# A reserve in the list scheduler for operations of attention and out-projection whose operands are not yet there

## The chip, the cores and the metric

The kernel runs on one core of a Trainium2 chip. The core has five engines that work side by side, each through its own instruction stream in the order in which the program was written: TensorE (PE: matmuls, and the weight loads that the profile lists as PEld), VectorE (DVE), ScalarE (ACT), GpSimd (POOL) and SyncE (SP, which here issues the DMAs). The metric is the device time of one execution in microseconds.

## What is computed

One layer of a hybrid decoder for 1024 tokens of width 1024, in fp32, cut here to its skeleton:

```python
xn = rms_norm(x, norm1_g)
proj = xn @ w_in                                   # ONE input projection
q, k, v, p_rw = jnp.split(proj, [512, 1024, 1536], axis=-1)
attn = dilated_attention(q, k, v, ...)             # 8 heads; windows (128,1) (512,4) (2048,16)
attn = rms_norm(attn, attn_out_g)                  # per head
rwkv = rwkv7_time_mix(p_rw, ...)                   # 8 heads; a recurrence over the tokens
mixed = jnp.concatenate([attn, rwkv], axis=-1)
x = x + mixed @ w_out                              # ONE out-projection
xn2 = rms_norm(x, norm2_g)
x = x + (silu(xn2 @ w_gate) * (xn2 @ w_up)) @ w_down
```

## The kernel before

All large products are split into a high and a low half in a reduced fp32 type and made of three passes of 128x512 matmuls (high x high, high x low, low x high). In the program's names an "h" or "l" at the end of a tile is such a half: `woh`, `wol` are the out-projection's weights, `mh`, `ml` the transposed mixed rows, `oph`, `opl` feed-forward weights, `B11h`, `B21h` the normalised rows of the feed-forward part.

The program is not written in the order in which it runs. Each piece of work is a generator (a *stream*) with a rank; it yields operations, waits on marks, and requests for PSUM banks. The class `Flow` keeps a model clock for each engine, and for each tile the model time at which it is written and read. `ready` (line 180) gives the earliest model time r at which the head of a stream can start: not before its engine is free, and not before its operands are there. `run` takes, at every step, the stream with the smallest r; where several could start by the model's present time, the one of the lowest rank. `issue` moves the clocks on and `emit` (line 235) writes the instruction down. So every engine instruction of the profile has the line L235, and what runs in which order is the outcome of this choice. On the chip each engine then works its list strictly in that order and waits at the head of it.

The program goes through these stages (times from the start of the span):

- **0 to about 550 us.** The input projection (rank 9), and beside it the preparation and the RWKV recurrence (ranks 3 to 3.6). The recurrence is a serial chain: 8 pairs of heads ("units"), 8 chunks each; on PE one step is `chain<-S,ra`, `chain<-Rb,M`, `chain<-VS,kbT`, `chain<-Ub,M`, with short DVE and ACT operations between.
- **550 to 600.** The input projection is done; the recurrence of the last unit runs beside the first attention items. `attend` (ranks 8.2 and up, several workers) takes a group of query blocks at a time: scores `<-kk,qv` on PE, bias and maximum on DVE, exponentials on ACT (`sb`), transposes `<-cs,sb`, copies to `pt`, `<-pt,vv` on PE.
- **600 to 770.** Attention, and the first of 384 out-projection matmuls (`outproj`, rank 9.5) as work that can stand in between. The out-projection has 16 blocks of 24 matmuls: round 0 (blocks 0 to 7) takes the RWKV half of the mixed rows, round 1 (blocks 8 to 15) the attention half. `mix_T` (rank 7.7) transposes the rows of a block on PE and splits them on ACT and DVE into `mh`, `ml`; `add_up` (7.8) adds a block to `acc` on DVE.
- **770 to 845.** `finish` (7.9) normalises the attention rows, a part at a time on ACT, DVE and POOL; round 1 needs it. Behind the last part of it `norms2` and `combine` (8.05) make the eight row blocks of the feed-forward's input.
- **845 to the end.** The feed-forward part (ranks 20 and above).

Of the kernel before, what the change touches and what calls it, by code (L numbers as in the profile page):

```python
# [48 lines left out]


LATE, SWITCH = 300, 100
OWN = {"PE": 0, "ACT": 100, "DVE": 130, "POOL": 95, "SP": 900}


# [49 lines left out]
class Flow:  # L104
# [73 lines left out]
                self.scan(s.head)  # L178

    def ready(self, s):  # L180
        op = s.head
        if isinstance(op, Wait):
            if any(m not in self.marks for m in op.marks):
                return None
            return max((self.marks[m] for m in op.marks), default=0.0)
        if isinstance(op, Get):
            t, n = sorted(self.free[op.kind].values()), op.n or 1
            return t[n - 1] if len(t) >= n else None
        r = self.clk.get(op.eng, 0.0)
        if op.eng == "SP":  # L190
            r = max(r, self.clk.get("queues", 0.0) - 3000)
        for keys, which in ((op.rd, 0), (op.wr, 0), (op.wr, 1)):
            for k in keys:
                if k in self.slots:
                    for e, t in self.slots[k][which].items():
                        if e != op.eng or (e == "SP" and (keys is op.rd or which)):
                            r = max(r, t + LAG[e] + (60 + LATE if op.eng == "PE" else 0))
                        elif keys is op.rd and which == 0:
                            r = max(r, t + OWN[e])
        return r  # L200

    def issue(self, s, r):
# [34 lines left out]
    def run(self, until):  # L237
        while True:
            best = None
            for s in self.streams:  # L240
                self.advance(s)
            held = {}
            for s in self.streams:
                if s.done:
                    continue
                r = self.ready(s)
                if r is None:
                    continue
                if isinstance(s.head, Op):
                    eng = s.head.eng  # L250
                    if eng in held and max(r, self.now) + s.head.cost > held[eng]:
                        continue
                    if eng in HOLD and s.rank == 3.1 and self.now < r <= self.now + HOLD[eng]:
                        held[eng] = min(r, held.get(eng, r))
                if best is None or r < best[0]:
                    best = r, s
                    if r <= self.now:
                        break
            self.streams = [s for s in self.streams if not s.done]
            if all(s.done for s in until):  # L260
                return
            assert best, [(s.gen.__name__, s.head.marks) for s in self.streams if isinstance(s.head, Wait)]
            self.now = max(self.now, best[0])
            self.issue(best[1], best[0])


@with_exitstack
# [1592 lines left out]
```

## Time and profile before

| | us |
|---|---|
| three runs | 1490.73, 1492.36, 1492.68 |
| their median | 1492.36 |
| the profiled execution | 1501.24 |
| its span (first to last instruction) | 1499.4 |
| PE busy in the span | 1426.3 (95%) |
| DVE, ACT, POOL busy | 801.1, 714.3, 539.8 |

The profile comes from one execution, whose own time is 8.9 us above the median of the runs. A row of the trace has the start of an instruction, its length, engine and line, the operation with output and inputs, and in brackets the time the engine sat idle before it and what ended that. Rows of equal instructions in a run are joined (x4). The granted clock of PE is given as a share of 2.4 GHz.

### The profile page before, as it was taken

The page shows a single profiled execution, that of the slowest core. Times are in us where ns is not written, and L with a number is a line of the kernel's source. Part 1 is how long each engine was busy: PE and PEld are TensorE (multiplying, and loading weights), DVE is VectorE, ACT ScalarE, POOL GpSimd, SP SyncE. Part 2 cuts the span into 40 slices and gives each one's busy share as a digit, 9 for nine tenths or more (in the row PEclk, how much of TensorE's full clock was granted, in tenths as well). Part 3 has the DMA queues.
Part 4 walks back from the last instruction along what each step waited for, and adds up shares of the span by engine and source line. Part 5 has one row for each costly group of instructions (what it writes and reads, how often), then busy time and mean ns, then how long its engine had stood idle before and what let it go on. Part 6 is the DMA issues. An engine that isn't in the chain of part 4 may idle for free. (4 is left out here: it accounts for less than half of the span.)

```text
span 1499.4 us, 24765 instructions
## 1 busy us (share of the span) xinstructions
PE 1426.3 (95%) x8710; PEld 1155.9 (77%) x8710; DVE 801.1 (53%) x1799; ACT 714.3 (48%) x1768; POOL 539.8 (36%) x564
## 2 busy tenths in 40 slices
PE   8999989999999986799999899999999999999999
PEld 5677767777778865688888678888888888888887
DVE  5456677657656337666776734443444434334334
ACT  5434556576676775555855433333333333333332
POOL 4432344255645451422454733444444440000000
PEclk8999999999999988799999999999999999999999
DMA  5343222323323344998521222222222224445443
GB/s 192 108 120 75 65 82 78 99 76 110 115 87 103 105 150 125 276 248 224 151 63 50 84 78 85 85 83 79 75 79 80 85 77 134 148 148 197 148 148 126
DMA packets 199789, 173.83 MB, mean 116 GB/s; under 512 B 39025, under 2 KB 150897, under 8 KB 199666
## 3 DMA queue, kind: packets, MB, share of 16 engines
q1 hardware_dynamic: 199666, 172.26, 38.3%
q8 instruction: 69, 1.13, 0.3%
q14 instruction: 54, 0.44, 0.1%
HBM read 130.26 MB, written 37.75 MB: 112 GB/s over the span
## 5 line engine op out<-in xcount | busy, mean ns | idle before, releaser
L235 ACT ACTIVATE oph<-fraw 128x512 fp32r<-128x512 f32 x208 | 126.3, 627 | 228.7 <-PE chain L235 97.9
L235 POOL TENSOR_TENSOR opl<-fraw,oph 128x512 fp32r<-128x512 f32 x76 | 99.6, 1315 | 220.6 <-PE bank L235 71.3
L235 DVE TENSOR_TENSOR opl<-fraw,oph 128x512 fp32r<-128x512 f32 x132 | 87.5, 689 | 143.6 <-ACT oph L235 143.6
L235 ACT ACTIVATE oph<-sw 128x512 fp32r<-128x512 f32 x80 | 50.6, 632 | 179.4 <-DVE sw L235 71.5
L235 POOL TENSOR_TENSOR inlo<-inraw,inhi 128x512 fp32r<-128x512 f32 x62 | 82.2, 1326 | 84.8 <-ACT inhi L235 70.6
L235 PE MATMUL bank<-opl,oph 128*128 128x512 f32 x176 | 68.5, 389 | 0.0
L235 PE MATMUL bank<-oph 128*128 128x512 f32 x176 | 68.5, 389 | 0.0
L235 PE MATMUL bank<-oph,opl 128*128 128x512 f32 x176 | 68.5, 389 | 0.0
L235 DVE TENSOR_TENSOR opl<-sw,oph 128x512 fp32r<-128x512 f32 x80 | 56.0, 699 | 21.0 <-ACT oph L235 17.2
L235 DVE TENSOR_TENSOR uu<-bank,uu 128x512 f32<-128x512 f32 x20 | 13.8, 692 | 81.7 <-PE bank L235 81.7
L235 DVE SCALAR_TENSOR_TENSOR S<-chain,ec,Sp 64x64 f32<-64x64 f32 x112 | 31.6, 282 | 43.1 <-PE chain L235 38.5
L235 ACT ACTIVATE Ub<-chain 64x64 f32<-64x64 f32 x128 | 28.2, 220 | 54.6 <-DVE VS L235 52.4
L235 POOL TENSOR_TENSOR sw<-fraw 128x512 f32<-128x512 f32 x40 | 52.0, 1299 | 0.0
L235 ACT ACTIVATE Y<-chain 64x64 f32<-64x64 f32 x128 | 26.9, 212 | 51.1 <-DVE S L235 45.8
L235 ACT ACTIVATE inhi<-inraw 128x512 fp32r<-128x512 f32 x62 | 38.7, 624 | 16.7 <-DMA inraw<-in_w_in_dram 6.7
L235 DVE COPY Rb<-chain 64x64 f32<-64x64 f32 x128 | 28.9, 226 | 27.9 <-PE chain L235 25.4
L235 POOL TENSOR_TENSOR up<-up,sg 128x512 f32<-128x512 f32 x20 | 32.3, 1617 | 30.1 <-POOL sw L235 16.1
L235 ACT ACTIVATE sb<-sb,mx 128x256 f32<-128x256 f32 (+3 forms) x64 | 36.2, 567 | 14.4 <-DVE mx L235 14.3
L235 PEld LDWEIGHTS bank<-oph,opl 128*128 128x128 f32 x176 | 33.0, 188 | 6.9
L235 PEld LDWEIGHTS bank<-oph 128*128 128x128 f32 x176 | 33.0, 188 | 6.8
L235 PEld LDWEIGHTS bank<-opl,oph 128*128 128x128 f32 x176 | 33.0, 188 | 6.8
L235 POOL TENSOR_TENSOR rsf<-smf,nhalf 128x8 f32<-128x8 f32 x16 | 26.6, 1662 | 31.6 <-DVE smf L235 31.3
(494 smaller groups left out, 4228.6 us busy)
## 6 DMA issues: line engine op xcount, KB each, us to landing
fraw<-in_w_down_dram SPq DMA_DIRECT2D x88, 256.0 KB, 2.8
inraw<-in_w_in_dram SPq DMA_DIRECT2D x62, 256.0 KB, 2.9
fraw<-in_w_gate_dram SPq DMA_DIRECT2D x48, 256.0 KB, 3.7
fraw<-in_w_up_dram SPq DMA_DIRECT2D x48, 256.0 KB, 3.0
fraw<-h_d SPq DMA_DIRECT2D x44, 256.0 KB, 2.9
h_d<-up SPq DMA_DIRECT2D x42, 256.0 KB, 2.1
rkv_d<-stage SPq DMA_DIRECT2D x24, 256.0 KB, 2.9
xt<-in_x_dram SPq DMA_DIRECT2D x8, 512.0 KB, 7.3
```

The costliest lines, as they stand in the source:

```text
L235: op.fn(*op.a, **op.k)
```

## The change

For an operation of a stream with a rank from 7 up to (not including) 10, on any engine but SP, whose operands come later than its engine is free, `ready` notes a second number, `when`, 400 ns behind r. `run` compares streams by `when`, where there is one, and by r otherwise; what is chosen is still issued at r. So out of several operations the one whose operands are there already is taken before one whose operands come within the next 400 ns of model time, and before one whose operands came in the model after its engine fell free. Ranks 7 to 10 are the loads of the out-projection's weights, `mix_T`, `add_up`, `finish`, `norms2`, `combine`, `attend`, the input projection and the out-projection. The recurrence (3 to 3.6) and the feed-forward streams (20 and above) have no reserve of their own, and no wait or bank request has one.

```diff
@@ -49,6 +49,8 @@
 LATE, SWITCH = 300, 100
+
+SLACK, SLACKED = 400, (7, 10)
 OWN = {"PE": 0, "ACT": 100, "DVE": 130, "POOL": 95, "SP": 900}
@@ -178,7 +180,9 @@
     def ready(self, s):
+
         op = s.head
+        s.when = None
@@ -186,7 +190,7 @@
-        r = self.clk.get(op.eng, 0.0)
+        r = free = self.clk.get(op.eng, 0.0)
@@ -197,6 +201,8 @@
+        if op.eng != "SP" and SLACKED[0] <= s.rank < SLACKED[1] and r > free:
+            s.when = r + SLACK
         return r
@@ -252,16 +258,17 @@
-                if best is None or r < best[0]:
-                    best = r, s
-                    if r <= self.now:
+                when = s.when or r
+                if best is None or when < best[0]:
+                    best = when, s, r
+                    if when <= self.now:
                         break
@@
-            self.now = max(self.now, best[0])
-            self.issue(best[1], best[0])
+            self.now = max(self.now, best[2])
+            self.issue(best[1], best[2])
```

The number of instructions of each engine is the same; their order differs, and with it which PSUM bank a product takes (the names `bank`, `mm`, `chain` at the left). Three places follow. In these rows `emit` has the line L235 before and L241 after.

First, PE in the last unit of the recurrence, at its fifth chunk: from `VS,kbT` to the next `S,ra`, the first twelve of the 22 rows that this is before:

```order
L235 MATMUL chain_6507<-VS,kbT 128x128
L235 MATMUL chain_6507<-Ub_116,M 128x128
L235 MATMUL bank_6597<-cs,sb_6444 128x128 x2
L235 MATMUL bank_6610<-pt_6577,vv 64x256
L235 MATMUL bank_6610<-pt_6577,vv 128x256
L235 MATMUL bank_6610<-pt_6577,vv 64x256
L235 MATMUL bank_6622<-cs,sb_6446 128x128 x3
L235 MATMUL mm_6632<-cs,sb_6447 128x128 x4
L235 MATMUL bank_6658<-cs,sb_6447 128x128 x3
L235 MATMUL bank_6610<-pt_6611,vv 128x256
L235 MATMUL bank_6610<-pt_6611,vv 64x256
L235 MATMUL bank_6610<-pt_6611,vv 128x128
```

and the same stretch, whole, after:

```order
L241 MATMUL chain_6501<-VS,kbT 128x128
L241 MATMUL chain_6501<-Ub_116,M 128x128
L241 MATMUL mm_6585<-cs,sb_6441 128x128 x2
L241 MATMUL bank_6608<-pt_6583,vv 128x256
L241 MATMUL bank_6608<-pt_6583,vv 64x256
L241 MATMUL bank_6608<-pt_6583,vv 128x256
L241 MATMUL bank_6608<-pt_6583,vv 64x256
L241 MATMUL chain_6588<-S_111,ra 128x128
```

Of 33 attention instructions that stood between the two steps 6 are left; the others stand in the next two steps of the recurrence and, 17 of them, behind its last instruction.

Second, PE behind the last instruction of attention, where `mix_T` transposes the rows of out-projection block 12 (`cs,O`). Before, the end of block 10, then the transposes, then block 11 (of 24 matmuls, whose first two are shown), behind which block 12 comes:

```order
L235 MATMUL mm_9181<-woh_8911,mh 128x512
L235 MATMUL mm_9181<-wol_8912,mh 128x512
L235 MATMUL mm_9181<-woh_8911,ml 128x512
L235 MATMUL bank_9212<-cs,O_6437 128x128
L235 MATMUL bank_9212<-cs,O_6438 128x128
L235 MATMUL bank_9212<-cs,O_6439 128x128
L235 MATMUL bank_9212<-cs,O_6440 128x128
L235 MATMUL mm_9207<-woh_8772,mh 128x512
L235 MATMUL mm_9207<-wol_8773,mh 128x512
```

After: the end of block 11, the transposes of blocks 12 and 13, and at once block 12:

```order
L241 MATMUL chain_9182<-wol_8703,mh 128x512
L241 MATMUL chain_9182<-woh_8702,ml 128x512
L241 MATMUL mm_9218<-cs,O_6434 128x128
L241 MATMUL mm_9218<-cs,O_6435 128x128
L241 MATMUL mm_9218<-cs,O_6436 128x128
L241 MATMUL mm_9218<-cs,O_6437 128x128
L241 MATMUL bank_9236<-cs,O_6434 128x128
L241 MATMUL bank_9236<-cs,O_6435 128x128
L241 MATMUL bank_9236<-cs,O_6436 128x128
L241 MATMUL bank_9236<-cs,O_6437 128x128
L241 MATMUL bank_9245<-woh_8547,mh 128x512
```

Between the last instruction of attention and the first matmul of block 12 there stood 60 out-projection matmuls (36 of them ahead of the transposes of block 12); now there are 10, all ahead of the transposes. Of the 384 matmuls 228 stood ahead of the end of attention, and 278 do now.

Third, PE at the end of the out-projection, where `norms2` transposes the normalised rows (`cs,nxn`) and the first feed-forward matmul (`B11h,oph`) follows. Before, the last of these transposes, with out-projection matmuls on both sides:

```order
L235 MATMUL chain_9473<-wol_8826,mh 128x512
L235 MATMUL mm_9483<-cs,nxn_9422 128x128 x4
L235 MATMUL chain_9473<-woh_8825,ml 128x512
L235 MATMUL chain_9473<-woh_8875,mh 128x512
L235 MATMUL chain_9473<-wol_8876,mh 128x512
```

After:

```order
L241 MATMUL mm_9473<-wol_8703,mh 128x512
L241 MATMUL mm_9473<-woh_8702,ml 128x512
L241 MATMUL chain_9489<-cs,nxn_9452 128x128 x4
L241 MATMUL bank_9498<-cs,nxn_9478 128x128 x4
L241 MATMUL bank_9510<-cs,nxn_9452 128x128 x4
L241 MATMUL bank_9519<-cs,nxn_9478 128x128 x4
L241 MATMUL chain_9549<-B11h,oph 128x512 x4
```

Before, 31 out-projection matmuls stood between the last transposes of `norms2` and the feed-forward's first matmul; now the transposes of the last two row blocks stand directly ahead of it.

## Rows read from the trace of the kernel before

**Rows 1.** The page: busy time, share, count; the chain that ended last.

```profile
PE 1426.3 (95%) x8710; PEld 1155.9 (77%) x8710; DVE 801.1 (53%) x1799; ACT 714.3 (48%) x1768; POOL 539.8 (36%) x564
...
PE 41%; DVE 0%; issue 0%
```

**Rows 2.** Table of windows: PE, PEld, DVE, ACT, POOL busy; PEclk, DMA share, GB/s.

```profile
900.00:1000.00 100.00, 100.00 (x437) 81.76 (x436) 41.21 (x64) 31.89 (x52) 40.69 (x32) 1.00 0.26 79
...
540.00:600.00 60.00, 41.82 (x234) 34.56 (x233) 35.62 (x115) 36.96 (x131) 13.31 (x14) 0.83 0.42 124
600.00:660.00 60.00, 50.91 (x288) 43.16 (x288) 38.84 (x132) 33.94 (x106) 22.97 (x23) 0.85 0.97 273
660.00:770.00 110.00, 103.78 (x679) 90.53 (x679) 81.21 (x293) 76.31 (x242) 43.16 (x80) 0.94 0.65 166
770.00:811.00 41.00, 41.00 (x207) 33.95 (x206) 27.24 (x49) 19.50 (x36) 16.71 (x27) 1.00 0.23 65
811.00:845.00 34.00, 26.98 (x132) 21.38 (x130) 27.47 (x34) 21.84 (x43) 24.90 (x21) 0.97 0.24 75
...
840.00:860.00 20.00, 16.02 (x64) 12.62 (x65) 15.74 (x22) 8.47 (x16) 15.25 (x12) 0.83 0.26 77
```

**Rows 3.** Timeline, end of the recurrence: start, length, engine, operation [idle before].

```profile
576.09 0.29 DVE L235 SCALAR_TENSOR_TENSOR S<-chain,ec,Sp 64x64 f32<-64x64 f32 x1
...
579.26 0.38 PE L235 MATMUL chain<-S,ra 128*128 128x128 f32 x2
...
600.08 0.48 PE L235 MATMUL chain<-cs,sb 128*128 128x128 f32 x1 [5.43 <-ACT sb L235]
```

**Rows 4.** Timeline of PE, 678 to 746: its waits for a head's queries.

```profile
689.01 1.39 PE L235 MATMUL mm<-kk,qv 128*128 128x128 f32 x6 [2.03 <-DMA qv<-qh_d]
...
745.32 0.66 PE L235 MATMUL chain<-kk,qv 128*128 128x128 f32 x4 [1.81 <-ACT qv L235]
```

**Rows 5.** Timeline of PE at the end of attention.

```profile
769.08 0.40 PE L235 MATMUL chain<-wol,mh 128*128 128x512 f32 x1
769.31 0.40 PE L235 MATMUL chain<-woh,ml 128*128 128x512 f32 x1
769.54 0.38 PE L235 MATMUL bank<-cs,sb 128*128 128x128 f32 x2
```

**Rows 6.** Timelines of DVE, PE and ACT: `finish`, then transposes and split of block 12.

```profile
772.06 0.29 DVE L235 TENSOR_TENSOR O<-O,agb 128x128 f32<-128x128 f32 x1
...
775.53 0.28 DVE L235 TENSOR_TENSOR O<-O,agb 128x128 f32<-128x128 f32 x1
...
778.48 0.60 PE L235 MATMUL bank<-cs,O 128*128 128x128 f32 x4
...
779.11 1.08 ACT L235 ACTIVATE mh<-bank 128x512 fp32r<-128x512 f32 x1 [4.84 <-PE bank L235]
...
780.23 1.10 DVE L235 TENSOR_TENSOR ml<-bank,mh 128x512 fp32r<-128x512 f32 x1 [0.28 <-ACT mh L235]
```

**Rows 7.** Timelines of ACT, DVE and PE: `norms2`, `combine`, first feed-forward products.

```profile
788.25 0.60 ACT L235 ACTIVATE B11h<-chain 128x512 fp32r<-128x512 f32 x1 [1.15 <-PE chain L235]
...
789.20 0.69 DVE L235 TENSOR_TENSOR B11l<-chain,B11h 128x512 fp32r<-128x512 f32 x1
...
811.33 1.10 PE L235 MATMUL bank<-B11h,oph 128*128 128x512 f32 x4
...
812.14 2.47 DVE L235 SCALAR_TENSOR_TENSOR nxn<-acc,nrs,g2bc 128x1024 f32<-128x1024 f32 x2
...
837.00 0.63 PE L235 MATMUL mm<-cs,nxn 128*128 128x128 f32 x4 [2.33 <-DVE nxn L235]
...
844.99 1.22 PE L235 MATMUL chain<-T1h,oph 128*128 128x512 f32 x2 [3.98 <-ACT T1h L235]
```

## Prediction

> **What bounds the kernel now.** I read the page first, then the table of windows, then PE's timeline where that table shows PE idle. The page has PE busy for 1426.3 of 1499.4 us, and the chain that ended last is all PE [rows 1]; so the time is PE's work plus PE's idle time, and an order that changes neither changes nothing. The table of windows says where idle time is left [rows 2]. From 900 to 1000 us PE is busy for 100.00 of 100 at a granted clock of 1.00 (2.4 GHz), and this is so for nearly all of the feed-forward part: nothing can be had there. Idle time stands in four stretches. 540 to 600 (18.2 us idle, clock 0.83) is the last unit of the serial recurrence. 600 to 660 (9.1 us, clock 0.85) has the DMA engines at 0.97: heads come in no faster than they are carried. 660 to 770 (6.2 us, clock 0.94) is attention proper. From 770 to 811 PE has no idle time at all, since the out-projection's rest fills it; from 811 to 845 it has 7.0 us.
>
> The change touches nothing but the order. In the feed-forward part it leaves the streams' own order as it is, so I cost that part at nothing; its cover is PE's own queue, which there never runs dry [rows 2].
>
> **The change, part by part.**
>
> *The dense stage, 0 to 550.* Counted in the order, the PE work between one step of the recurrence and the next, converted with the lengths of the rows, is 1.74 us before and 1.75 after ahead of `Rb`, 2.21 and 2.22 ahead of `VS,kbT`, 2.42 and 2.38 ahead of `S,ra` (means over some 53 steps each). Those differences, times 53, are 0.5 and 0.5 us of loss and 2.1 of gain. Value 0; bounds -1 and +2.
>
> *The last unit of the recurrence.* The state `S` of the fifth chunk is finished at 576.09 + 0.29 = 576.38, but its matmul starts at 579.26 [rows 3]: it stood behind the 33 attention instructions of the first fence, so 2.9 us were lost there. Now 6 stand there. That is a gain of 2.9 at most. It is not that much: the other instructions stand in the next two steps, or behind the chain, and there are three places at which an ACT or DVE operation of attention now stands ahead of one of the recurrence, each of the size of an ACT or DVE row of a few tenths, 1 us together. Also the chain's end does not release PE: after it PE waits 5.43 us for the first `sb`, until 600.08 [rows 3], and that waits for DVE to end the post-processing of the recurrence. The 17 instructions that now stand behind the last step fall into this hole and cost nothing there. I take -0.6, near nought, since most of what left one step comes back in the next two; bounds -2.9 and +1.
>
> *Attention, 660 to 770.* 50 out-projection matmuls (278 - 228) move ahead of the end of attention. One takes 769.31 - 769.08 = 0.23 us of PE [rows 5], so 11.4 us of work is put into this stage. By itself that makes attention end 11.4 us later and leaves 11.4 us less behind it: no gain. It gains what idle time it fills. The idle time there is 110.00 - 103.78 = 6.2 us [rows 2], and more than half of that is two waits for queries that have just been loaded, 2.03 and 1.81 us [rows 4]; ahead of the first stand matmuls of a later block now, and ahead of the second, scores of another head, so both can be filled. Against a full gain: the gaps that the order leaves in dependent work are not longer. From the last `pt,vv` of an item to its next transposes the PE work in between is 1.44 us before, 1.40 after, on the mean of 40; from transposes to their `pt,vv` 1.96 and 1.92, of 32. The additional matmuls went into gaps from scores to transposes (7.34 to 9.04), which were long enough. So I count the two waits and some 0.5 us besides, -4.4; bounds -6.2 (all idle time) and 0 (as much is lost at new heads of queues). 600 to 660 I leave at nought, the same number of matmuls standing ahead of its waits.
>
> The clock: at 0.94 on the mean over 110 us between 1.2 and 2.4 GHz, 0.06 x 2 x 110 = 13 us ran at the lower level [rows 2], which costs at most half of that, 6.6 us. PE falls there after waits: the 20 us from 840, which begin with a wait of 3.98 us, have 0.83 [rows 2, 7]. I give the clock no term, with 0 and -6.6 for its bounds, since the gaps do not get shorter. The Trainium skill (TensorE: Matmul & The Clock Gate, "HAM oscillation") says that bursts of matmuls with waits in between lose the high clock again and again, and that a steadier supply keeps it. The trace agrees as far as those 20 us go; by that rule the term would be -4.4 - 6.6 = -11.0 if the supply became steady, and a new hole elsewhere would cost more than its length.
>
> *Behind attention: block 12.* The last attention instruction on PE is that of 769.54 [rows 5]. Block 12 needs a part of `finish`, its transposes, and the split into `mh` and `ml`. Before, 36 matmuls, 8 us, ran ahead of its transposes and 24 more behind them: everything was hidden. Now 10 matmuls, 2.3 us, stand ahead, and none behind. The split shows fully: from the transposes at 778.48 to the end of `mh` at 780.19 are 1.7 us, to the end of `ml` 2.9 [rows 6]; the transposes of block 13 cover 0.6 and two matmuls 0.5 more. That is some 1.2 us at least. In addition the transposes of block 13 stand ahead of block 12 and need the next part of `finish`, which came 775.53 + 0.28 - 769.54 = 6.3 us after the end of attention [rows 5, 6]; less 2.3 and 0.6 (the transposes of 12), 3.4 us of wait, and up to 4.5 with the rest of the split. The parts of `finish` come somewhat earlier against the end of attention now, since their head's work ends earlier. I take +2.5; bounds +1.2 and +4.5. Queued behind it on PE are the out-projection and with it `add_up`, `norms2` and all of the feed-forward part.
>
> *At the end of the out-projection.* Before, the transposes of `norms2` ran between out-projection matmuls, and the feed-forward's first matmul followed the last of these without a gap (811.33) [rows 7]. Now those of the last two row blocks stand directly ahead of it. Their results are split by four pairs of ACT 0.60 and DVE 0.69 [rows 7]; 0.6 for the first transposes, 0.6 ACT and 4 x 0.69 DVE are 4.0 us, less 2.2 of transposes that PE does anyway: +1.8, with the way from engine to engine +2. Bounds 0 (the 4.0 beside the wait that follows) and +3.7 (the second normalisation on DVE late too, 2.47 / 2 = 1.2 more, and 0.5). The 7.0 us of waits from 811 to 845 stay: they end with `T1h`, 844.99, which follows the `combine` of 812.14 by 32.9 us [rows 7], and this `combine` moves with the end of the out-projection.
>
> **Sum.** 0 - 0.6 - 4.4 + 2.5 + 2.0 = -0.5 us. On the profiled execution, 1501.24, that is 1500.7; its span is 1499.4, the 1.8 us around it do not change. The runs' median lies 8.9 us below the profiled execution, so I apply the difference to it: 1492.36 - 0.5 = 1491.9.
>
> **The rivals.**
>
> *A, the idle time is really filled:* the added matmuls take all of the 6.2 us and half of the low clock's price, 3.3, and the places behind attention cost their lower ends: -0.6 - 6.2 - 3.3 + 1.2 = -8.9, 1483.5. For it speaks that 11.4 us of independent work is more than the idle time there; against it, the gaps counted above.
>
> *B, slower, the lost cover:* attention ends later by the whole 11.4 us, since on an engine that works in order each matmul put ahead of an attention instruction delays it by 0.23 unless it would have waited as long; and the tail has become too short to hide `finish` and the splits: 0 - 0.6 + 4.5 + 3.7 = +7.6, 1500.0, and up to 3.4 more if the clock falls as it did from 840 (0.17 x 2 x 20 / 2). It decides from the point where less than 4 us is gained in attention. For it speaks that from 770 to 811 PE was busy throughout, so there was nothing to mend; against it, that the waits from 811 to 845 might absorb part of it.
>
> *C, the order changes but no idle time does:* 1492.4. New holes as large as those filled elsewhere.
>
> **How the numbers follow.** Forecast 0.40, A 0.30, B 0.25, C 0.05. The forecast's own terms can be off by more than 3 us in either direction (all lower bounds together are -15.5, all upper ones +11.2): of its 0.40 I give 0.24 to within 0.2% (3 us, about what a measurement of this kernel can tell from no change), 0.09 to faster, 0.07 to slower. So faster 0.39, same 0.29, slower 0.32. The range takes in A's and B's times, 1483 to 1501; the ends at which all bounds fall on one side lie outside it, in the 2 in 10.
>
> **What would show it.** The chunk of 579.26 starts within 1 us of its `S`. In the windows of attention the idle time falls from 6.2 us to about 2, and attention ends 6 to 8 us later than 769.54. Behind it PE waits at the transposes of blocks 12 and 13 and at the first matmul of block 12, some 2.5 us, where there was none, and again some 2 us ahead of the first feed-forward matmul. From `combine` on everything is as before, moved as a whole. I am wrong if attention ends at 769.5 or earlier (then A or better), or if it ends 11 us later with as much idle time as before (B), or if the feed-forward part itself changes its length.

## The result

The change makes the kernel slower: 1510.61 us against 1492.34, both medians of four runs, a ratio of 1.0124 (95% interval 1.0107 to 1.0142). The forecast was 1491.9.

The page of the kernel after shows the same work, in a longer span (1507.3 us):

```profile
span 1507.3 us, 24759 instructions
...
PE 1427.2 (95%) x8710; PEld 1152.5 (76%) x8710; DVE 803.8 (53%) x1799; ACT 714.4 (47%) x1768; POOL 538.1 (36%) x564
```

PE's busy time is that of [rows 1] within 1 us, so against that profile what was added is idle time. But the two spans differ by 7.9 us only, though the medians differ by 18. The profile ahead of the prediction lies above its own runs, so the kernel before was profiled once more (first experiment below), and that second profile, span 1490.0, is what I compare with from here on. Its page has, for PE:

```profile
PE 1421.0 (95%) x8710; PEld 1150.2 (77%) x8710; DVE 800.7 (54%) x1799; ACT 715.4 (48%) x1768; POOL 540.6 (36%) x564
```

Against it, 11.1 of the 17.3 us between the spans are idle time of PE (80.1 us instead of 69.0), and 6.2 are busy time: the same 8710 matmuls took longer. Table of windows of the kernel after, columns as in [rows 2]:

```profile
540.00:600.00 60.00, 45.36 (x241) 36.95 (x239) 34.85 (x110) 37.76 (x130) 14.99 (x15) 0.84 0.44 129
600.00:660.00 60.00, 50.85 (x303) 43.58 (x303) 41.33 (x145) 35.71 (x110) 22.52 (x24) 0.87 0.99 282
660.00:777.00 117.00, 111.01 (x713) 96.14 (x713) 83.46 (x293) 76.82 (x239) 42.80 (x82) 0.96 0.58 151
777.00:812.00 35.00, 31.63 (x160) 25.33 (x159) 23.70 (x43) 16.02 (x32) 14.89 (x21) 1.00 0.28 79
812.00:851.00 39.00, 28.63 (x129) 22.93 (x129) 29.96 (x34) 24.84 (x49) 27.47 (x24) 0.87 0.22 68
...
900.00:1500.00 600.00, 599.99 (x2626) 492.57 (x2625) 238.29 (x366) 191.89 (x316) 146.72 (x110) 1.00 0.34 109
```

Attention, 660 to 777, is idle for 6.0 us, as much as [rows 2] shows for 660 to 770; what was put in did not displace idle time. (The second profile of the kernel before has 4.6 in 660 to 760.) The stretch that had no idle time, 770 to 811, now has 3.4 us in 777 to 812. And the stretch of `combine`, 7.0 us idle in 34 before, has 10.4 in 39, at a clock of 0.87 instead of 0.97. From 900 us on PE never waits, as before.

The milestones on PE. First the kernel before, second profile: last unit's first `S,ra`, end of the recurrence, last attention instruction, first feed-forward product, first product with `T1h`:

```profile
546.93 0.49 PE L235 MATMUL chain<-S,ra 128*128 128x128 f32 x2 [0.29 <-DVE S L235]
...
590.38 0.49 PE L235 MATMUL chain<-Ub,M 128*128 128x128 f32 x2 [0.43 <-ACT Ub L235]
...
760.20 0.38 PE L235 MATMUL bank<-cs,sb 128*128 128x128 f32 x2
...
801.99 1.10 PE L235 MATMUL bank<-B11h,oph 128*128 128x512 f32 x4
...
835.62 2.08 PE L235 MATMUL chain<-T1h,oph 128*128 128x512 f32 x4 [3.98 <-ACT T1h L235]
```

and the kernel after, with the waits that are new:

```profile
551.26 0.49 PE L241 MATMUL chain<-S,ra 128*128 128x128 f32 x2 [0.29 <-DVE S L241]
...
592.92 0.49 PE L241 MATMUL chain<-Ub,M 128*128 128x128 f32 x2 [0.29 <-ACT Ub L241]
...
777.48 0.38 PE L241 MATMUL mm<-cs,sb 128*128 128x128 f32 x2
...
781.15 0.33 PE L241 MATMUL mm<-cs,O 128*128 128x128 f32 x1 [0.66 <-DVE O L241]
...
782.93 0.33 PE L241 MATMUL bank<-cs,O 128*128 128x128 f32 x1 [1.13 <-DVE O L241]
...
783.91 0.50 PE L241 MATMUL bank<-woh,ml 128*128 128x512 f32 x1 [0.18 <-DVE d L241]
...
809.55 1.50 PE L241 MATMUL bank<-cs,nxn 128*128 128x128 f32 x12 [0.67 <-DVE nxn L241]
...
811.79 1.20 PE L241 MATMUL chain<-B11h,oph 128*128 128x512 f32 x4 [0.74 <-ACT B11h L241]
...
842.06 1.11 PE L241 MATMUL chain<-cs,nxn 128*128 128x128 f32 x4 [4.73 <-DVE nxn L241]
...
850.58 2.07 PE L241 MATMUL bank<-T1h,oph 128*128 128x512 f32 x4 [3.27 <-ACT T1h L241]
...
854.27 2.07 PE L241 MATMUL bank<-T1l,oph 128*128 128x512 f32 x4 [1.61 <-DVE T1l L241]
```

From these two fences: the last unit starts 4.3 us later and takes 1.8 less (41.7 instead of 43.5); attention takes 14.7 more (184.6 instead of 169.8), of which 11.4 are the 50 matmuls put into it, so 3.3 are lost; the stretch to the first feed-forward product takes 7.5 less, where 11.4 less work is in it, so 3.9 are lost; from there to the first `T1h` 5.2 more (38.8 instead of 33.6); and from there to the end of the span 2.3 more. The sum, 4.3 - 1.8 + 3.3 + 3.9 + 5.2 + 2.3, is 17.2 of the 17.3 us between the spans.

The windows of attention alone, in the second profile of the kernel before and in the kernel after, show what the 3.3 us are:

```profile
590.38:760.20 169.82, 152.07 (x975) 130.09 (x976) 124.79 (x439) 110.90 (x350) 68.36 (x105) 0.94 0.77 204
592.92:777.48 184.56, 167.40 (x1043) 143.99 (x1044) 130.21 (x448) 115.01 (x358) 67.34 (x107) 0.93 0.69 188
```

PE's idle time is 0.6 us less there (17.2 instead of 17.8); its busy time grew by 15.3 us, 3.9 more than the matmuls put in.

### The profile page after: what moved, and what is told of

The parts are those of the page before. It is cut to its first block, busy times and chain, and to the rows that moved or that the text cites. A ratio compares the mean times of both kernels' runs of the same rounds, so it can differ in the third digit from the quotient of the medians.

```text
span 1507.3 us, 24759 instructions
## 1 busy us (share of the span) xinstructions
PE 1427.2 (95%) x8710; PEld 1152.5 (76%) x8710; DVE 803.8 (53%) x1799; ACT 714.4 (47%) x1768; POOL 538.1 (36%) x564
## 3 DMA queue, kind: packets, MB, share of 16 engines
q8 instruction: 69, 1.13, 0.3%
## 5 line engine op out<-in xcount | busy, mean ns | idle before, releaser
L241 ACT ACTIVATE oph<-fraw 128x512 fp32r<-128x512 f32 x208 | 126.1, 628 | 222.2 <-PE bank L241 99.3
L241 POOL TENSOR_TENSOR opl<-fraw,oph 128x512 fp32r<-128x512 f32 x76 | 100.2, 1322 | 214.4 <-PE mm L241 67.1
L241 DVE TENSOR_TENSOR opl<-fraw,oph 128x512 fp32r<-128x512 f32 x132 | 87.6, 689 | 143.5 <-ACT oph L241 143.5
L241 ACT ACTIVATE oph<-sw 128x512 fp32r<-128x512 f32 x80 | 50.6, 632 | 179.8 <-DVE sw L241 71.6
L241 POOL TENSOR_TENSOR inlo<-inraw,inhi 128x512 fp32r<-128x512 f32 x62 | 81.6, 1316 | 89.3 <-ACT inhi L241 67.8
L241 PE MATMUL bank<-oph 128*128 128x512 f32 x176 | 68.6, 390 | 0.0
L241 PE MATMUL bank<-oph,opl 128*128 128x512 f32 x176 | 68.5, 389 | 0.0
L241 PE MATMUL bank<-opl,oph 128*128 128x512 f32 x176 | 68.5, 389 | 0.0
L241 DVE TENSOR_TENSOR opl<-sw,oph 128x512 fp32r<-128x512 f32 x80 | 55.0, 687 | 21.3 <-ACT oph L241 17.5
L241 DVE TENSOR_TENSOR up<-bank,uu 128x512 f32<-128x512 f32 x40 | 27.7, 691 | 56.3 <-PE bank L241 54.8
L241 DVE TENSOR_TENSOR uu<-bank,uu 128x512 f32<-128x512 f32 x20 | 13.8, 692 | 81.7 <-PE bank L241 81.7
L241 DVE SCALAR_TENSOR_TENSOR S<-chain,ec,Sp 64x64 f32<-64x64 f32 x112 | 31.6, 282 | 48.3 <-PE chain L241 43.9
L241 ACT ACTIVATE Ub<-chain 64x64 f32<-64x64 f32 x128 | 28.1, 219 | 60.1 <-DVE VS L241 58.2
L241 POOL TENSOR_TENSOR sw<-fraw 128x512 f32<-128x512 f32 x40 | 51.7, 1292 | 0.0
L241 ACT ACTIVATE Y<-chain 64x64 f32<-64x64 f32 x128 | 26.9, 212 | 48.9 <-DVE S L241 46.2
L241 DVE COPY Rb<-chain 64x64 f32<-64x64 f32 x128 | 29.0, 226 | 35.3 <-PE chain L241 33.0
L241 ACT ACTIVATE inhi<-inraw 128x512 fp32r<-128x512 f32 x62 | 38.7, 624 | 13.5 <-PE mm L241 9.6
L241 POOL TENSOR_TENSOR up<-up,sg 128x512 f32<-128x512 f32 x20 | 32.7, 1633 | 30.4 <-POOL sw L241 16.4
L241 ACT ACTIVATE sb<-sb,mx 128x256 f32<-128x256 f32 (+3 forms) x64 | 36.3, 568 | 10.6 <-DVE mx L241 10.3
L241 PEld LDWEIGHTS bank<-oph 128*128 128x128 f32 x176 | 33.0, 188 | 7.2 <-DVE acc L241 0.4
L241 PE MATMUL bank<-ra,kb 64*64 64x128 f32 x512 | 38.3, 277 | 0.0
L241 PEld LDWEIGHTS bank<-oph,opl 128*128 128x128 f32 x176 | 33.0, 188 | 6.9
```

What stands on the lines that cost most here:

```text
L241: op.fn(*op.a, **op.k)
```

## The experiments

All runs have the kernel before beside them on the same chip. What differs is one line of `ready`: to which operations the reserve applies. This table has the medians, the ratios to the kernel before, the number of out-projection matmuls that the order puts ahead of the end of attention (`n`), and the stages as differences to the second profile of the kernel before, read off PE's timeline as above: A the end of the recurrence, B from there to the end of attention, C from there to the first feed-forward product, D from there to the first `T1h`, E from there to the end. B, C: each matmul of `n` beyond 228 moves 0.23 us from C to B.

| run | reserve on | us | ratio (95%) | n | A | B | C | D | E |
|---|---|---|---|---|---|---|---|---|---|
| after | 7 to 10 | 1510.6 | 1.0124 (1.0107, 1.0142) | 278 | +2.5 | +14.7 | -7.5 | +5.2 | +2.3 |
| e0 | none | 1493.8 | 1.0004 (0.9986, 1.0022) | 228 | 0 | 0 | 0 | 0 | 0 |
| e1 | 7 to 10 but 8.05 | 1504.8 | 1.0084 (1.0063, 1.0105) | 278 | +1.9 | +15.5 | -9.1 | +2.1 | +2.3 |
| e2 | 8.05 (norms2, combine) | 1498.4 | 1.0039 (1.0024, 1.0054) | 228 | 0.0 | -0.5 | 0.0 | +4.0 | +1.9 |
| e3 | attend | 1495.9 | 1.0026 (1.0011, 1.0040) | 274 | -4.9 | +10.4 | -4.4 | +0.5 | +0.3 |
| e4 | attend, early | 1490.2 | 0.9989 (0.9972, 1.0006) | 228 | -3.1 | +1.0 | -0.1 | 0.0 | -0.3 |
| e5 | attend, late | 1497.7 | 1.0036 (1.0020, 1.0052) | 274 | -2.4 | +8.6 | -4.2 | +0.5 | +0.7 |
| e6 | 9 to 10 | 1500.0 | 1.0049 (1.0032, 1.0065) | 237 | +2.5 | +7.0 | -1.4 | 0.0 | +0.6 |
| e7 | 7 to 8 | 1498.9 | 1.0037 (1.0021, 1.0053) | 198 | +1.0 | -3.4 | +12.6 | 0.0 | +1.1 |
| e8 | 8.05, T1h put back | 1498.2 | 1.0039 (1.0021, 1.0058) | 228 | +0.3 | -2.4 | 0.0 | +3.0 | +3.5 |
| e9 | none, T1h swapped | 1495.9 | 1.0015 (1.0000, 1.0030) | 228 | -0.3 | +0.8 | 0.0 | +1.8 | +2.8 |
| e10 | 9 (input projection) | 1496.0 | 1.0026 (1.0008, 1.0043) | 228 | +1.6 | +1.5 | 0.0 | 0.0 | +1.5 |
| e11 | 9.5 (out-projection) | 1495.1 | 1.0024 (1.0006, 1.0042) | 237 | -2.4 | +6.2 | -1.2 | 0.0 | +1.1 |
| e12 | 8.05, opl put back | 1503.0 | 1.0076 (1.0059, 1.0094) | 228 | -1.9 | +1.0 | -0.1 | +11.7 | 0.0 |
| e13 | 8.05, both put back | 1503.2 | 1.0073 (1.0049, 1.0096) | 228 | -1.5 | +2.7 | 0.0 | +9.9 | +0.1 |
| e14 | attend, n held at 228 | 1496.1 | 1.0024 (1.0013, 1.0036) | 228 | -5.5 | +4.8 | 0.0 | 0.0 | -0.1 |
| e15 | 7 to 10, PE alone | 1507.9 | 1.0106 (1.0082, 1.0129) | 195 | +2.6 | -4.5 | +16.2 | 0.0 | +2.5 |
| e16 | 7 to 10, but PE | 1512.8 | 1.0144 (1.0116, 1.0172) | 263 | -3.1 | +17.7 | -2.6 | +5.5 | +2.9 |
| e17 | attend, early (again) | 1491.5 | 0.9999 (0.9983, 1.0016) | 228 | -3.1 | 0.0 | 0.0 | 0.0 | +1.1 |

How much of a difference is the order's: A hangs on when the first step of the recurrence starts too, which is anywhere from 131.6 to 136.1 us; B, where attention keeps its order (e2, e8, e9, e10, e12, e13), is between -2.4 and +2.7, but the first profile of the kernel before has a B of +7.3 against the second; D, where combine keeps its order, agrees within 0.1 us when C does; E, where combine keeps its order, is between -0.3 and +2.5. So D speaks by itself, a B of less than 3 us says nothing alone, and one of less than 7 is not safe. The stages are those of one profiled execution each. It lies within 2.8 us of the median of its run, but for e7 (4.2 above) and e14 (5.2 below).

**e0, the kernel before again.** No edit.

> The kernel before, profiled once more, since its trace (span 1499.4, execution 1501.24) lies 8.9 us above the median of its runs and the two spans (1499.4, 1507.3) differ by 7.9 us where the medians differ by 18.3. If the first trace held something that the usual execution has not, the new span is about 1490 and the stretch in which it is shorter shows it. If profiling itself adds the 9 us, the new span is about 1499 again.

Measured: span 1490.0. It is the first profile that held something more, and it stands ahead of the end of attention, which comes at 760.20 instead of 769.54 [rows 5]; from there to the end both traces agree within 0.1 us. Of these 9.3 us, 2.0 stand ahead of the recurrence's end (592.42 and 590.38) and 7.3 in attention. Its table of windows:

```profile
600.00:660.00 60.00, 53.43 (x316) 44.39 (x314) 41.08 (x145) 34.05 (x106) 25.15 (x26) 0.93 1.02 281
660.00:760.00 100.00, 95.43 (x645) 83.18 (x645) 76.45 (x268) 74.18 (x234) 41.20 (x77) 0.97 0.68 174
```

6.6 us idle at a clock of 0.93 where [rows 2] has 9.1 at 0.85; 4.6 idle at 0.97 in 100 us where it has 6.2 at 0.94 in 110. So not all of the 7.3 us are waits: over the whole of attention the first profile has 20.7 us idle at a clock of 0.90, the second 17.8 at 0.94. The wait of 2.03 us for a DMA [rows 4] is not in this trace at all; that of 1.81 for ACT is, with 1.9.

**e1 and e2, norms2 and combine without, and alone.**

```
e1:  SLACKED[0] <= s.rank < SLACKED[1] and s.rank != 8.05
e2:  s.rank == 8.05
```

> The change without the reserve on rank 8.05 (norms2 and combine); attention, finish, mix_T, add_up and both projections keep it. Theory 1 (the loss is made in combine, whose two workers now go in lockstep on DVE and POOL, so that the third and fourth row block start 6 us later): about 7 us less than the change, near 1503. Theory 2 (the loss comes from the order ahead of the feed-forward part, where attention's instructions stand behind more out-projection): no gain, 1508 to 1512.

> The kernel before with the reserve on rank 8.05 alone (norms2 and combine). Theory 1: slower than before by 5 to 8 us, 1497 to 1500. Theory 2: as before, 1492.

Measured: e1 gains 5.8 us on the change, and e2 loses 6.6 on the kernel before; both are near theory 1's figures. But e1, with no reserve on `norms2` and `combine`, keeps 4.4 us of the change's 7.5 in D and E, so that part of what is lost there comes from the order ahead of `combine`; by what way is not shown. In e2 the recurrence, attention and the out-projection are those of the kernel before (A, B, C within 0.5), and D and E are 5.9 us longer. So the order of `norms2` and `combine` alone costs some 6 us. How, is told by PE and POOL of e2; the last row is the kernel before (e0), whose first feed-forward product runs at 801.99 and that of e2 at 801.52:

```profile
832.06 1.12 PE L241 MATMUL chain<-cs,nxn 128*128 128x128 f32 x4 [6.32 <-DVE nxn L241]
...
839.10 1.22 PE L241 MATMUL mm<-T1h,oph 128*128 128x512 f32 x2 [3.27 <-ACT T1h L241]
...
815.87 1.30 POOL L241 TENSOR_TENSOR opl<-fraw,oph 128x512 fp32r<-128x512 f32 x1 [2.65 <-ACT oph L241]
817.13 1.29 POOL L241 TENSOR_TENSOR tt<-B21h,tt 128x512 f32<-128x512 f32 x1
...
812.22 1.30 POOL L235 TENSOR_TENSOR tt<-B21h,tt 128x512 f32<-128x512 f32 x1 [0.63 <-DVE T1l L235]
```

PE waits 6.32 us for the normalised rows of the third row block of `combine` where it waited 2.34 (2.33 in [rows 7]). The third block needs a tile that the first gives back with its last split, `T4l`; and in the first block the fourth term (`tt<-B21h,tt`) runs 5 us later on POOL. (In e2 that split, at 822.31, ends at 824.09, and ACT starts the third block's `nxn` at 824.18.) In front of the fourth term stands an `opl` of the feed-forward's weights that waits 2.65 us for its other half on ACT: the scheduler took it first, and on the chip it was not ready. What a list in strict order has at its head holds all that is behind it.

**e8, e9, e12, e13: which instruction of combine it is.** ACT's table load and first SiLU stand ahead of the first block's `T1h` in e2 (814.12 us on ACT, against 810.49 in e0). e8 puts that back in e2, e9 makes this one swap in the kernel before, e12 puts the `opl` on POOL back in e2, and e13 both.

```
e8:   combine, behind T3h:        + yield Mark(("h13", i))
      gates, ahead of the SiLU:   + if p == 0: yield Wait(("h13", 4))
e9:   combine, ahead of T1h:      + if i == 4: yield Wait(("sg0", 0))
e12:  combine, behind tt<-B21h:   + yield Mark(("t4", i))
      prepare_ff, 8th operand, between its ACT and its POOL half:   + yield Wait(("t4", 4))
```

> The reserve on rank 8.05 alone, as in the earlier run that took 1498.4, with one operation put back by a mark: the first SiLU of the feed-forward part (ACT, with its table load of 1.28 us) waits until combine's T1h and T3h of row block 4 have been written down, as they stand in the kernel before. Theory 1 (a ready operation of low rank on ACT overtakes the chain that PE will wait for, and that is the first 3 us of the loss): 1494 to 1496. Rival (the lockstep of the two workers on DVE and POOL makes the loss): 1498, no gain.

> The kernel before, with the one swap alone: T1h of row block 4 waits until the first SiLU has been written down. Theory 1: slower than before by 2 to 4 us, 1494 to 1495. Rival: as before, 1491 to 1492.

> The reserve on rank 8.05 alone (1498.4 by itself), with the POOL order put back: the feed-forward split opl that had moved ahead of combine's fourth term (tt<-B21h,tt of row block 4) waits for it by a mark. In the run with rank 8.05 alone this opl sat on POOL for 2.65 us waiting for its ACT half, and combine's tt behind it ran at 817.1 instead of about 812 after the same start. Theory (an operation that is there by the model's clocks is not there on the chip, and on POOL it blocks the chain that the third row block waits for): 1493 to 1495, and the wait for nxn ahead of 6 us becomes 3. Rival (neither ACT nor POOL by itself): 1498.

> Both put back: combine's T1h and T3h of row block 4 ahead of the first SiLU on ACT, and the opl behind combine's tt on POOL. Theory: the stretch from the first feed-forward product to the first T1h is 33.6 to 34.5 us as before (37.6 with the reserve), 1491 to 1493. Rival: 1496 to 1498.

Measured: e8 has no gain (1498.2 to e2's 1498.4), e9 a loss of 2 to 4 us (ratio 1.0015, medians 3.9 us apart) whose interval begins at 1.0000 (D alone, +1.8, is clear), e12 and e13 lose 5 us more than e2. So the swap on ACT costs something where it is made alone, but neither swap gains anything when it is put back. PE of e12 shows why a single operation can't be put back:

```profile
830.95 1.11 PE L241 MATMUL chain<-cs,nxn 128*128 128x128 f32 x4 [5.74 <-DVE nxn L241]
...
837.40 1.09 PE L241 MATMUL chain<-cs,nxn 128*128 128x128 f32 x4 [4.48 <-DVE nxn L241]
...
846.31 2.07 PE L241 MATMUL mm<-T1h,oph 128*128 128x512 f32 x4 [6.97 <-ACT T1h L241]
```

The first wait is as long as before, a second of 4.48 us follows, and `T1h` comes 7 us later than in e2: with the marks the scheduler chose another order for all that follows, in which the second block's last split stands behind the third block's normalisation on DVE. What is shown is that the order within `combine` costs 6 us, and that four other orders of it cost between 4.6 and 11.7 in D and E. Which of its instructions carries the loss of the change stays open.

**e3, e4, e5, e17: attend.**

```
e3:       8.1 <= s.rank < 9
e4, e17:  not self.late and 8.1 <= s.rank < 9
e5:       self.late and 8.1 <= s.rank < 9       # late: set when the recurrence's streams have ended
```

> The reserve on attend alone (ranks 8.2 and up, under 9). 274 out-projection matmuls stand ahead of the end of attention (228 before, 278 with the change), and combine stands as before. Theory 1: no loss, 1488 to 1493. Theory 2: most of the loss, 1500 to 1510.

> The reserve on attend alone, and only until the recurrence's streams have ended; from there on the rule is that of the kernel before (228 out-projection matmuls ahead of the end of attention, as before). With the reserve on attend throughout the recurrence ended at 585.5 and the first transposes behind it ran at 594.2, against 590.4 and 598.1 of the kernel before in its second profile. Theory 1 (PE is what bounds the stages behind, so these 4 us go through to the end): 1487 to 1489, faster than before. Rival (the heads' loads, at a DMA share of about 1 from 600 to 700 us, set the pace and eat it): 1491 to 1492.

> The complement: the reserve on attend alone, and only from the end of the recurrence's streams on (274 out-projection matmuls ahead of the end of attention). Theory 1 (the loss of the change's attend part lies behind the recurrence, where the added matmuls gain about 1 us of idle time and the shortened tail costs 6): recurrence ends at about 590 as before, 1496 to 1499. Rival (the order in attention costs nothing by itself): 1491 to 1493.

> The reserve on attend alone until the recurrence's streams have ended, a second time, since the first run left open whether it is faster (0.9989 of before, 0.9972 to 1.0006). If the recurrence's shorter end goes through: 0.997 to 0.999 again, with an interval that ends below 1 with both runs together. If not: 0.9995 to 1.001.

Measured: e3 loses 4 us, neither of its two theories. e5, at 1497.7 where its theory 1 has it, shows where: 274 - 228 = 46 matmuls, 10.5 us, move into attention, which gets 8.6 longer, so it gains 1.9; and the tail gets only 4.2 shorter, so it loses 6.3. PE of e5 behind the end of attention (766.41):

```profile
772.55 0.33 PE L242 MATMUL chain<-cs,O 128*128 128x128 f32 x1 [2.24 <-DVE O L242]
...
774.34 0.33 PE L242 MATMUL mm<-cs,O 128*128 128x128 f32 x1 [1.13 <-DVE O L242]
...
775.66 0.80 PE L242 MATMUL bank<-woh,ml 128*128 128x512 f32 x1 [0.52 <-DVE ml L242]
```

The transposes of the out-projection wait for `finish`, and the matmul for its split: the rival B of the prediction. The early half, e4, ends the recurrence 3 us earlier (1.5 us of it, and all of it in e17, is an earlier first step) and looked like a gain; run again, e17, it is 0.9999. With both runs no gain is shown.

**e14, the matmuls held back.**

```
outproj, n == 9, second half:   + yield Wait(*[("values", h, i) for h in (6, 7) for i in (6, 7)])
```

> The reserve on attend alone (1495.9 by itself, 274 out-projection matmuls ahead of the end of attention), and the second half of out-projection block 9 waits until the last item of attention is done, so that 228 matmuls stand ahead as in the kernel before and the tail has its old length. Theory (the reserve on attend gains in the recurrence's end and in attention, and all its loss is the cover that the tail gives away): the end of attention by some 3 us earlier than before, the tail at 41.8 us, 1486 to 1489. Rival (the gain in attention was the matmuls themselves, idle time returns where they stood): 1491 to 1494.

Measured: the tail has its old length (C and D 0.0), and the recurrence ends early, but attention is 4.8 us longer with the same 228 matmuls in it, and the whole is at 1496.1, above both theories. Its profiled execution, at 1490.9, is the fastest of its twelve, so the stages do not hold all of the loss. No gain of the reserve in attention is left over: with more matmuls in it the tail loses, without them attention does.

**e6, e10, e11: the projections, and e7, the small operations.**

```
e6:  9 <= s.rank < 10        e10: s.rank == 9        e11: s.rank == 9.5        e7: 7 <= s.rank < 8
```

> The reserve on ranks 9 to 10 alone, the input projection and the out-projection. The recurrence ended 2 us later with the change than before (592.9 against 590.4) and 5 us earlier with attend alone, so something else in the change delays it by 7 us. Theory 1 (it is the input projection's reserve): the recurrence ends at 593 or later, total 1495 or more. Rival (it is the two together): as before, 1491 to 1493.

> The reserve on rank 9 alone, the input projection. With ranks 9 to 10 the run was at 1500.0; the recurrence took 457.3 us from its first step to its last instead of 455.8, and the stretch from there to the end of attention 176.8 instead of 169.8, with only 9 out-projection matmuls (2 us) more in it. Theory 1 (the input projection carries the loss, by what it leaves for the time behind it): 1497 or more. Rival (the out-projection carries it): 1492 to 1494.

> The complement: the reserve on rank 9.5 alone, the out-projection. Theory 1: 1491 to 1494. Rival: 1497 or more, with waits on PE in attention that the kernel before has not.

> The reserve on ranks 7 to 8 alone: loads of weights, mix_T, add_up, finish. 198 out-projection matmuls stand ahead of the end of attention instead of 228. If the order of these few operations matters: attention ends about 30 x 0.23 = 7 us earlier and the tail is longer by as much, total as before, 1491 to 1493. If blocks of the out-projection wait for their transposes and splits: 1495 and more.

Measured: e6 loses 8.7 us, shared between its halves: e10 loses some 4, e11 some 3. In e10 the last unit of the recurrence starts at

```profile
551.73 0.49 PE L241 MATMUL chain<-S,ra 128*128 128x128 f32 x2 [0.29 <-DVE S L241]
```

that is 416.6 us behind the first step (135.17), where the kernel before has 412.4 (134.58 to 546.93) and the change 418.2 (133.02 to 551.26). The windows from first step to last unit, kernel before (second profile), after, and e10:

```profile
134.58:546.93 412.35, 394.45 (x3573) 315.05 (x3573) 253.38 (x642) 266.55 (x792) 192.46 (x194) 1.00 0.32 96
...
133.02:551.26 418.24, 399.85 (x3575) 315.95 (x3575) 252.53 (x642) 263.73 (x787) 189.58 (x192) 0.99 0.32 95
...
135.17:551.73 416.56, 398.30 (x3576) 314.38 (x3576) 253.52 (x642) 263.99 (x787) 189.86 (x192) 1.00 0.32 95
```

PE was idle for hardly longer in that time (18.3 us in e10, 18.4 in the change, 17.9 before), and it did the same work: but for two of the input projection, the matmuls are the same, and none of attention is among them. They took 3.9 us more of PE's busy time in e10 and 5.4 in the change; why, is not shown. What does it is the reserve on the input projection's PE instructions: the five profiles that have it (the change, e1, e6, e10, e15) have 416.6 to 418.2 us here, all others 411.1 to 414.4, e16 among them with 411.4. Part is given back: the last unit then takes 40.3 us in e10 instead of 43.5, so that the recurrence, first step to end, takes 456.8 us instead of 455.8. Over all profiles that is 456.8 to 459.9 us with this reserve and 452.0 to 457.2 without. So e10 and e11 lie between their theories: both projections share the loss. In e11 attention gets 6.2 longer with 9 matmuls (2.1 us) more. In e7 fewer matmuls stand in attention (30 x 0.23 = 6.9 us), which gets only 3.4 shorter, and the tail grows by 12.6: PE waits 2.9 us there for splits of the weights, 1.57 at the most, and the transposes of one more block stand in it. That is 5.7 us more than was moved into it, and e7's second theory holds.

**e15 and e16, by engine.**

```
e15: op.eng == "PE" and SLACKED[0] <= s.rank < SLACKED[1]
e16: op.eng not in ("SP", "PE") and SLACKED[0] <= s.rank < SLACKED[1]
```

> The change with the reserve on PE alone (ranks 7 to 10). 195 out-projection matmuls stand ahead of the end of attention (228 before, 278 with the change), and combine stands on DVE as before. Theory (the loss comes from the engines that run the chains between PE's instructions: ACT, DVE and POOL): 1492 to 1498, less than half of the change's 18 us. Rival (the loss is PE's order): 1503 or more.

> The complement: the reserve on ACT, DVE and POOL alone. 263 matmuls ahead of the end of attention, combine in lockstep as with the change. Theory: 1504 to 1512, most of the loss. Rival: 1492 to 1500.

Measured: each half alone loses about what both lose (16 us e15, 21 e16, 18 the change), and the two sums of parts (by stream, e2, e3, e6 and e7: 27; by engine: 37) are well above the whole. So the parts' losses can't be added up to the change's. e16, at 1512.8, is just above theory's 1504 to 1512, and its D, +5.5, is as long as the change's. e15's is the rival's, but by another way: PE alone puts fewer matmuls into attention (195), and then stands in the tail, where two matmuls wait for the low halves of the weights, split on POOL:

```profile
761.41 0.50 PE L241 MATMUL bank<-wol,mh 128*128 128x512 f32 x1 [1.06 <-POOL wol L241]
...
765.55 0.79 PE L241 MATMUL bank<-wol,mh 128*128 128x512 f32 x1 [3.17 <-POOL wol L241]
```

No version beats the kernel before.

## Why the prediction was wrong

The steps in the prediction's order, measured as the change less the second profile of the kernel before:

| step | predicted (bounds) | measured |
|---|---|---|
| dense stage | 0 (-1, +2) | +4.3 |
| last unit of the recurrence | -0.6 (-2.9, +1) | -1.8 |
| attention | -4.4 (-6.2, 0) | +3.3 |
| block 12 and the end of the out-projection | +4.5 (+1.2, +8.2) | +3.9 |
| combine and behind | 0 | +7.5 |
| sum | -0.5 | +17.2 |

**Combine** is the step that failed most, and it was in no sum and no rival ("The 7.0 us of waits from 811 to 845 stay"), only among the signs of being wrong ("if the feed-forward part itself changes its length"). I had costed the feed-forward part at nothing, with PE's full queue for cover, and held combine for a chain that moves as a whole. But PE's queue does run dry there (that is what the 7.0 us were), and combine has the rank 8.05, inside the range of the change. Its DVE, ACT and POOL lists should have been laid beside those of before: first and second block go in step now, and the third starts later. e2 measures this reserve alone, 6 us in D and E; that e1 keeps 4.4 us there without it says that the order ahead of `combine` has a share, too.

**Attention** was counted as a gain by its idle time. The room was in part an accident: 9.4 us of the profiled execution are not in the second one, most of them in this stage, and one of the two waits that I filled was a DMA's of that execution alone. The other is not filled. It is there in the second profile and, longer, in the kernel after:

```profile
734.42 1.12 PE L235 MATMUL chain<-kk,qv 128*128 128x128 f32 x4 [1.87 <-ACT qv L235]
...
738.21 0.98 PE L241 MATMUL bank<-kk,qv 128*128 128x128 f32 x4 [2.80 <-ACT qv L241]
```

Over the whole stage PE's idle time fell by 0.6 us, not by 4.4. I noted that the profiled execution lay 8.9 us above the runs, and took the difference for something that lies over all. It did not; it stood where my gain was. What spoke against the gain, the gaps in dependent work that get no longer, was the better argument, and I let it take off 1.8 us of 6.2. The measured +3.3 lies beyond the upper bound, 0: for the worst I took that as much is lost as is filled. It is busy time, not idle time, and it is less than the 7.3 us by which two profiles of one program differ here, so its size is not safe. Beyond the matmuls put in, attention is 4 to 10 us longer in e11, e14 and e16, but not in e3 and e5, which have the reserve on `attend` alone (-0.1 and -1.9). Which operation's place makes it longer stays open.

**The dense stage** was costed by the PE work between one step of the recurrence and the next, as a mean, which had not changed. What failed is taking the length of that work as given: the same matmuls, but two, took 5.4 us more of PE's busy time in the change's order, with 0.5 us more idle time, and the last unit started 4.3 us later though PE had no other work ahead of it. That the input projection's reserve on PE does this is shown (e10, e15, e16); what makes the matmuls longer stays open.

**Right** was the tail, 3.9 us for 4.5: 3.4 of them are waits at the transposes of both blocks (0.66 and 1.13), at block 12 (0.18), at the last transposes of `norms2` (0.67) and ahead of the first feed-forward product (0.74), about where the prediction had them. Right was also the fifth chunk of the last unit, which starts right behind its state now instead of 2.9 us later:

```profile
577.97 0.29 DVE L241 SCALAR_TENSOR_TENSOR S<-chain,ec,Sp 64x64 f32<-64x64 f32 x1
...
578.32 0.49 PE L241 MATMUL chain<-S,ra 128*128 128x128 f32 x2 [0.66 <-DVE S L241]
```

But that the unit as a whole is 1.8 us shorter says little: it is 1.6 shorter in e2, too (41.9 instead of 43.5), where its order is that of the kernel before. The mechanism of rival B, that each matmul put ahead delays attention and leaves the tail without cover, is what e5 shows; its price, 7.6, was missing combine.

**The clock** had no term, and bounds (0 and -6.6) on the side of a gain only. The mean granted clock of the change's four runs is 0.974 or 0.975; in the runs of the kernel before, beside the experiments, its median is 0.981 or 0.982. In the two profiles compared it is 0.975 and 0.979 (0.973 in the first profile of the kernel before). An estimate from these: 0.025 x 2 x 1507.3 = 75 us ran at 1.2 GHz in the change and 0.021 x 2 x 1490.0 = 63 us in the kernel before, and the 13 us between them cost at most half, some 6 of the 17.3 us; PE's busy time is 6.2 us longer. The holes that the change made in PE's work thus seem to have cost more than their length; no run here varies the clock alone.

On the clock gate: by the Trainium skill's rule (TensorE: Matmul & The Clock Gate, HAM oscillation) the prediction let a hole cost more than its length. The windows 812 to 851 agree as to the direction, with 0.87 for 0.97 where PE's waits grew by 3.4 us.

## What to carry to other kernels

A list scheduler's rule that prefers what is ready by its own clocks reorders every engine that it touches; lay the lists of all engines side by side at each place where a chain is short of cover, also those behind the place that is meant, and above all where two workers share buffers. Idle time in one profile is room only if it is there in a second profile; when the profiled execution lies above its runs, find out first where. Work counted in instructions, with one length for each, is not time: the same matmuls in another order took up to 5 us longer here, and no wait showed it; compare the time from a chain's first step to its last as well.

## What was not expected of the hardware

An elementwise DVE instruction of combine that reads two tiles of SBUF, the on-chip memory, has two lengths. In the kernel before, second profile, and in the kernel after, the same split of 128x512:

```profile
818.81 1.77 DVE L235 TENSOR_TENSOR T4l<-tt,T4h 128x512 fp32r<-128x512 f32 x1
...
823.91 0.86 DVE L235 TENSOR_TENSOR T4l<-tt,T4h 128x512 fp32r<-128x512 f32 x1 [0.83 <-ACT T4h L235]
...
843.74 0.69 DVE L235 TENSOR_TENSOR T4l<-tt,T4h 128x512 fp32r<-128x512 f32 x1
...
836.58 3.44 DVE L241 TENSOR_TENSOR T4l<-tt,T4h 128x512 fp32r<-128x512 f32 x2
```

It takes 0.69 us, or 1.75 to 1.78, and now and then something between; the long ones lie where POOL runs elementwise work of its own, whose instructions are then 1.7 long instead of 1.3. In both traces together, 389 such instructions of `combine` and of the weights' splits have no 128x512 work of POOL beside them, and all take 0.68 or 0.69 us; the 18 of over 1.3 us all have 1.1 us or more of it beside them. Among those with less of it, up to 0.8 us, the longest takes 0.90. In the order after both of the first two are long. No run here varied that alone, so that POOL's work is the cause is only argued. The Trainium skill (GPSIMD Engine Reference, Specifications) says that GpSimd shares its SBUF interfaces with VectorE, which contends with DVE instructions of two SBUF inputs; that would fit, these having two. How much of combine's 6 us this is, stays open.
